# A gated-delta and mLSTM layer: branch a's gates projected beside branch b's, k's squares on ScalarE, two heads' w and state products in two banks

## The chip, the cores and the metric

One core of a Trainium2 chip runs the whole program. The metric is the device time of one execution in microseconds, the median of several executions. A profiled execution also leaves a trace; its span runs from the first to the last instruction.

## The reference

Two blocks follow each other on 256 tokens of width 1024. The first (two layers of token mixers and experts) is not touched. The second has two layers; in each, every product with a weight is over 1024 inputs:

```python
proj = x @ w_in      # q,k,v,o of branch a (mLSTM, 4 heads); q,k,v,z of branch b (gated delta, 8 heads); gate_a, gate_b
ha = headnorm(mlstm(qa, ka, va)) * sigmoid(oa)
q, k, v = silu(causal_conv(qkv_b))              # branch b; q, k then scaled by rsqrt(sum of squares + 1e-6)
# chunks of 64 tokens, per head: u, w from a triangular solve, then for each of 4 chunks
v_new = u - w @ S;  o = qe @ S + attn @ v_new;  S = S * g_end + kd.T @ v_new
hb = headnorm(o) * silu(zb)
y = sigmoid(gate_a) * (ha @ w_branch_a) + sigmoid(gate_b) * (hb @ w_branch_b)
x = layernorm(ALPHA * x + y @ w_out);  x = layernorm(ALPHA * x + ffn(x))
```

## The kernel before

Everything is in float32. A product with a weight matrix is made in `gemm_t` of three single-pass matmuls (lines L85 to L87): the weight tile `w` is split into a high and a low part `whl` (ScalarE copies the high part, L62, VectorE subtracts, L64), the activations are kept as such a pair (`xh`, `xl`). One call handles 256 output columns with 48 matmuls of 256 columns into one PSUM tile `acc`, and then an evacuation. Below, "projection matmul" is any of these. All other products (those in `gdn` and `mlstm`) are plain float32 matmuls, which the trace shows as two instructions each, transposes as one.

Branch b works on two heads at a time: a head pair `hp` holds its heads in the two halves of the 128 partitions (`halves`). `gdn_proj` projects q, k, v of a pair, applies the convolution, and GpSimd squares q and k (L1236, tiles `cva`). `gdn` then sums the squares over the 128 channels with matmuls against ones (`pss`, L1261), takes the reciprocal root, transposes k and v (`pk`, `pv`), scales k into `kt`, transposes it back (`pkT`), solves the triangular system in six levels (`pi`), makes u (`pu`) and w (`pw`, L1364), and walks the four chunks: `pO[:, 1]` is w times S (L1376), `vn` the new values (L1378), `pO[:, 0]` the output (L1380, L1393), `pS` the state product of each head (L1387), then VectorE updates S (L1389, L1391) and ScalarE takes the output and its squares out of PSUM (L1396, L1397). After the chunks comes the norm (L1406) and a transpose `pot` (L1409). PSUM tiles of a pair rotate through two banks (tag `ma` or `mb` by the parity of the pair).

`branches` makes the four gates of branch b (columns `GB`), the four products of hb with `w_branch_b`, and then by turns a gate of branch a (columns `GA`, into a tile `ta`) and a product of ha. The order of the steps is the string `ORDER2` (P and M: projections and core of branch a; G, Z and R: projections, gate and core of branch b; R0 to R3 twice, once a layer). That is the order of writing; a scheduler with its own timing then puts the instructions of each engine into their final order, and takes one that stands later when an earlier one has no free buffer or no data. Each engine executes its own list in that order.

Of the kernel before, what the change touches and what calls it, by code (L numbers as in the profile page):

```python
# [7 lines left out]
FT = mybir.dt.float32  # L8
FR = mybir.dt.float32r
I32 = mybir.dt.int32  # L10
AF = mybir.ActivationFunctionType
OP = mybir.AluOpType
# [31 lines left out]
def wload(E, parts, kn):  # L44

    nc = E.nc
    cols = sum(p.shape[1] for p in parts)
    w = E.wp.tile([128, kn, cols], FT, name="w", tag="w")
    o = 0
    for p in parts:  # L50
        n = p.shape[1]
        nc.sync.dma_start(w[:, :, o:o + n], p.rearrange("(k p) n -> p k n", p=128))
        o += n
    return w
# [18 lines left out]
def gemm_t(E, parts, xh, xl, evac, pool=None, tag="acc"):  # L73


    nc = E.nc
    j = 0
    for p in parts:
        for c in range(0, p.shape[1], 256):
            w = wload(E, [p[:, c:c + 256]], KC)  # L80
            ps = (pool or E.acc).tile([128, 2, 256], FT, name="acc", tag=tag)
            for b in range(2):
                h, lo = split(E, w[:, :, b * 128:(b + 1) * 128], [128, KC, 128])
                for k in range(KC):
                    nc.tensor.matmul(ps[:, b], h[:, k], xh[:, k], start=(k == 0), stop=False)  # L85
                    nc.tensor.matmul(ps[:, b], h[:, k], xl[:, k], start=False, stop=False)  # L86
                    nc.tensor.matmul(ps[:, b], lo[:, k], xh[:, k], start=False, stop=(k == KC - 1))  # L87
            evac(j, ps)
            j += 1
# [974 lines left out]
QA, KA, VA, OA, QB, KB, VB, ZB, GA, GB = 0, 512, 1024, 2048, 3080, 4104, 5128, 6152, 7192, 8216  # L1064
# [130 lines left out]
class G2:  # L1195
# [27 lines left out]
    def gdn_proj(self, hp):  # L1223
        E, nc, T, cw = self.E, self.E.nc, self.E.t2, self.cw
        z = Env()
        z.KQ = T.tile([128, 2, 4, 2, 64], FT, name="KQ")
        z.kr = T.tile([128, 4, 2, 64], FT, name="kr", bufs=1)
        z.vr = T.tile([128, 4, 2, 64], FT, name="vr", bufs=1)
        z.sq = []

        def ev(j, ps):
            dst = z.KQ[:, 1] if j == 0 else z.kr
            a = conv_piece(E, cw, j * 8 + 2 * hp, ps, dst)
            d2 = dst.rearrange("p c h t -> p (c h t)")
            z.sq.append(a.rearrange("p a b -> p (a b)"))
            nc.gpsimd.tensor_mul(z.sq[j], d2, d2)  # L1236
        gemm_t(E, [self.cols(QB + 256 * hp), self.cols(KB + 256 * hp)], self.xh, self.xl, ev)
        gemm_t(E, [self.cols(VB + 256 * hp)], self.xh, self.xl, lambda j, ps: conv_piece(E, cw, 16 + 2 * hp, ps, z.vr))
        return z
# [10 lines left out]
    def gdn(self, hp, z):  # L1250
        E, nc, m, C, T = self.E, self.E.nc, self.E.m, self.E.c2, self.E.t2
        gd, R, KQ = self.R["gd"], self.R, z.KQ
        p_ = "ab"[hp % 2]
        mt = "m" + p_
        halves = [slice(0, 64), slice(64, 128)]


        pss = m.tile([128, 2, 4], FT, name="pss", tag=mt)
        for j in range(2):
            for c in range(4):  # L1260
                nc.tensor.matmul(pss[:, j, c:c + 1], z.sq[j][:, c * 128:c * 128 + 128], C.ones[:, 0:1], start=True, stop=True)  # L1261
        nn = E.sm.tile([128, 8], FT, name="nn", tag="nn" + p_)
        nc.vector.tensor_scalar(nn, pss.rearrange("p a b -> p (a b)"), 1e-6, None, op0=OP.add)
        rr = E.sm.tile([128, 8], FT, name="rr", tag="rr" + p_)
        rsqrt(E, rr, nn, (128, 8), p_)
        qsc = E.sm.tile([128, 4], FT, name="qsc", tag="qsc" + p_)
# [1 line left out]
        rk = rr[:, 4:8]  # L1268


        pk = m.tile([128, 4, 128], FT, name="pk", tag=mt)
        pv = m.tile([128, 4, 128], FT, name="pv", tag=mt)
        for c in range(4):
            nc.tensor.transpose(pk[:, c], z.kr[:, c], C.id)
        for c in range(4):
            nc.tensor.transpose(pv[:, c], z.vr[:, c], C.id)
        kt = T.tile([128, 4, 128], FT, name="kt", bufs=1)
        nc.vector.tensor_mul(kt, pk, bc(rk, 128))
        vb = T.tile([128, 4, 128], FT, name="vb")
        nc.vector.tensor_mul(vb, pv, bc(gd[:, 1, hp], 128))  # L1280
# [2 lines left out]
        kd = T.tile([128, 4, 128], FT, name="kd")  # L1283
# [15 lines left out]
        ge = E.sm.tile([128, 2, 4], FT, name="ge", tag="ge" + p_)  # L1299
# [57 lines left out]
        u = vb  # L1357
        nc.scalar.activation(u, pu, AF.Copy)
        wT = kb.rearrange("p c (a b) -> p (c a) b", b=64).rearrange("p (h c) t -> p h c t", h=2)
        pws = []  # L1360
        for hpar, s in enumerate(halves):
            pw = m.tile([128, 4, 64], FT, name="pw", tag=mt)
            for c in range(4):
                nc.tensor.matmul(pw[:, c], kb[s, c], XY[s, 1, c], start=True, stop=True)  # L1364
            pws.append(pw)
        for hpar in range(2):
            nc.scalar.activation(wT[:, hpar], pws[hpar], AF.Copy)

# [1 line left out]
        ss = E.sm.tile([128, 4], FT, name="ss", tag="ss" + p_)  # L1370
        S = None
        for c in range(4):
            po = m.tile([128, 2, 128], FT, name="pO", tag=mt)
            if c:
                for hpar, s in enumerate(halves):
                    nc.tensor.matmul(po[s, 1], wT[:, hpar, c], S[:, hpar], start=True, stop=True, skip_group_check=True)  # L1376
                vn = T.tile([128, 128], FT, name="vn", tag="vn" + p_, bufs=1)
                nc.vector.tensor_sub(vn, u[:, c], po[:, 1])  # L1378
                for hpar, s in enumerate(halves):
                    nc.tensor.matmul(po[s, 0], qe[:, c, hpar], S[:, hpar], start=True, stop=False, skip_group_check=True)  # L1380
            else:
                vn = u[:, 0]
            if c < 3:
                Sn = T.tile([128, 2, 128], FT, name="S", tag="S" + p_, bufs=2)
                for hpar, s in enumerate(halves):
                    pS = m.tile([128, 128], FT, name="pS", tag=mt)
                    nc.tensor.matmul(pS, kd[s, c], vn[s], start=True, stop=True)  # L1387
                    if c:
                        nc.vector.scalar_tensor_tensor(Sn[:, hpar], S[:, hpar], ge[:, hpar, c:c + 1], pS, op0=OP.mult, op1=OP.add)  # L1389
                    else:  # L1390
                        nc.vector.tensor_copy(Sn[:, hpar], pS)  # L1391
            for s in halves:
                nc.tensor.matmul(po[s, 0], at[s, c], vn[s], start=(c == 0), stop=True, skip_group_check=True)  # L1393
            if c < 3:
                S = Sn
            nc.scalar.activation(u[:, c], po[:, 0], AF.Copy)  # L1396
            nc.scalar.activation(self.junk[:, 0:128], po[:, 0], AF.Square, accum_out=ss[:, c:c + 1])  # L1397


        nc.vector.tensor_mul(ss, ss, qsc)  # L1400
# [124 lines left out]
    def branches(self):  # L1525

        E, nc, T = self.E, self.E.nc, self.E.t2
        l = self.l
        self.yh = E.st.tile([128, 8, 256], FR, name="yh", tag="st")
        self.yl = E.st.tile([128, 8, 256], FR, name="yl", tag="st")  # L1530
        yb = []

        def gate(c0, p, t):
            gemm_t(E, [self.cols(c0 + 256 * p)], self.xh, self.xl,
                   lambda j, ps: nc.scalar.activation(t, ps, AF.Tanh, scale=0.5))

        def product(p):
            t = yb[p]
            gemm_t(E, [E.i["w_branch_b_2"][l, :, 256 * p:256 * p + 256]], self.hbh, self.hbl,
                   lambda j, ps: nc.vector.scalar_tensor_tensor(t, t, 1.0, ps, op0=OP.add, op1=OP.mult))  # L1540
        for p in range(4):
            t = E.rows.tile([128, 2, 256], FT, name="yb", tag="yg", bufs=3) if p < 3 else T.tile([128, 2, 256], FT, name="yb", tag="vb")
            yb.append(t)
            gate(GB, p, t)
        for p in range(4):
            product(p)
        for p in range(4):
            f = slice(2 * p, 2 * p + 2)
            t = T.tile([128, 2, 256], FT, name="ta", tag="gs")
            gemm_t(E, [self.cols(GA + 256 * p)], self.xh, self.xl,  # L1550
                   lambda j, ps: nc.scalar.activation(t, ps, AF.Tanh, scale=0.5))

            def ev(j, ps):
                y = T.tile([128, 2, 256], FT, name="cva")
                nc.vector.scalar_tensor_tensor(y, t, 1.0, ps, op0=OP.add, op1=OP.mult)
                nc.vector.tensor_add(y, y, yb[p])
                nc.scalar.activation(self.yh[:, f], y, AF.Copy, scale=0.5)
                nc.vector.scalar_tensor_tensor(self.yl[:, f], y, 0.5, self.yh[:, f], op0=OP.mult, op1=OP.subtract)
            gemm_t(E, [E.i["w_branch_a_2"][l, :, 256 * p:256 * p + 256]], self.hah, self.hal, ev)
# [310 lines left out]
```

## Time and profile before

| | |
|---|---|
| median of 3 executions | 2811.3 us (2809.31 to 2815.72) |
| profiled execution | 2815.0 us, span 2813.3 us |
| TensorE (PE) busy in the span | 2524.8 us, 90% |
| VectorE (DVE), ScalarE (ACT), GpSimd (POOL) busy | 1350.2, 821.7 and 239.6 us |
| mean granted clock of TensorE | 0.958 |

The share of busy time is a mean over both blocks. The second block starts at about 1520 us; its two layers are the stretches to read. PE's weight loads have a row of their own (PEld) and overlap the matmuls. A granted clock of 1.00 is 2.4 GHz, 0.50 is 1.2 GHz.

### The profile page before, as it was taken

What the parts mean: (1) busy time and instruction counts of PE and PEld (TensorE: products, weight loads), DVE (VectorE), ACT (ScalarE), POOL (GpSimd) and SP (SyncE); (2) the same over time, 40 slices, a digit from 0 to 9 for tenths busy, and PEclk for the clock granted to TensorE, in tenths of its full rate; (3) what the DMA queues carried; (4) which work ended last, traced back from release to release, by engine and by line L of the source; (5) the groups of instructions that cost most, each with busy time, mean ns of one, the idle gap of its engine ahead of it and who ended that gap; (6) DMA issues with size and microseconds to landing.
All of it is one profiled execution on the core that took longest, in us unless ns stands there. A gap on an engine that the chain in (4) does not pass through costs nothing.

```text
span 2813.3 us, 42526 instructions
## 1 busy us (share of the span) xinstructions
PE 2524.8 (90%) x17783; PEld 1736.5 (62%) x17783; DVE 1350.2 (48%) x2673; ACT 821.7 (29%) x1343; POOL 239.6 (9%) x309
## 2 busy tenths in 40 slices
PE   6999989988889998666667999999999999999998
PEld 4776733322227662111114988888997898879996
DVE  4446533232236562001103767456655677455765
ACT  2334310000014440000002434334444443334442
POOL 1000010000000001000000122000201031100200
PEclk8999999999999999998899998999999998999999
DMA  7534469999995468999997421335654431235553
GB/s 294 180 120 148 165 265 421 421 421 421 421 384 197 168 250 370 421 421 421 421 421 280 152 92 53 113 111 177 209 181 139 150 121 46 94 102 198 178 193 120
DMA packets 237460, 665.61 MB, mean 237 GB/s; under 512 B 11572, under 2 KB 165860, under 8 KB 182356
## 3 DMA queue, kind: packets, MB, share of 16 engines
q1 hardware_dynamic: 235428, 657.81, 61.4%
q0 software_dynamic: 1696, 4.59, 0.5%
q8 instruction: 140, 2.29, 0.3%
q10 hardware_dynamic: 144, 0.49, 0.1%
q14 instruction: 52, 0.43, 0.0%
HBM read 661.78 MB, written 1.05 MB: 236 GB/s over the span
## 4 chain that ended last, share of the span: by engine, by line
PE 60%; DMA 24%; issue 9%; DVE 4%; POOL 2%; ACT 1%; SPq 0%; DVEq 0%; ACTq 0%; POOLq 0%
DMA w<-in_exp_w_up 9%; DMA w<-in_exp_w_down 8%; PE acc L85 6%; PE acc L87 6%; PE acc L86 6%; DMA w<-in_exp_w_gate 6%; PE pj L317 3%; PE pj L319 3%; PE pj L318 3%; PE pgate L883 3%; PE pd L883 3%; PE pup L883 2%; PE pada L183 2%; PE psc L436 1%; PE psc L452 1%
## 5 line engine op out<-in xcount | busy, mean ns | idle before, releaser
L64 DVE TENSOR_TENSOR whl<-w,whl 128x1024 fp32r<-128x1024 f32 x376 | 469.0, 1251 | 297.6 <-ACT whl L62 296.7
L62 ACT ACTIVATE whl<-w 128x1024 fp32r<-128x1024 f32 x376 | 396.1, 1058 | 483.5 <-PE acc L87 245.0
L85 PE MATMUL acc<-xh,whl 128*128 128x256 f32 x1664 | 474.4, 285 | 0.8 <-DVE xh L1648 0.5
L86 PE MATMUL acc<-xl,whl 128*128 128x256 f32 x1664 | 471.1, 283 | 0.0
L87 PE MATMUL acc<-xh,whl 128*128 128x256 f32 x1664 | 470.5, 283 | 0.2
L85 PEld LDWEIGHTS acc<-xh,whl 128*128 128x128 f32 x1664 | 315.1, 189 | 10.4 <-issue 6.3
L86 PEld LDWEIGHTS acc<-xl,whl 128*128 128x128 f32 x1664 | 315.2, 189 | 5.0 <-issue 3.9
L87 PEld LDWEIGHTS acc<-xh,whl 128*128 128x128 f32 x1664 | 314.8, 189 | 5.3 <-issue 3.3
L883 PE MATMUL pup<-w,xg 128*64 128x512 f32 (+1 forms) x1024 | 223.6, 665 | 68.6 <-DMA w<-in_exp_w_up 68.6
L883 PE MATMUL pd<-w,ehT 128*64 128x512 f32 (+1 forms) x1024 | 208.3, 639 | 58.1 <-DMA w<-in_exp_w_down 41.0
L883 PE MATMUL pgate<-w,xg 128*64 128x512 f32 (+1 forms) x1016 | 215.2, 635 | 47.3 <-DMA w<-in_exp_w_gate 38.7
L883 PEld LDWEIGHTS pup<-w,xg 128*64 128x64 f32 (+1 forms) x1024 | 52.0, 129 | 231.1 <-DMA w<-in_exp_w_up 151.4
L883 PEld LDWEIGHTS pd<-w,ehT 128*64 128x64 f32 (+1 forms) x1024 | 52.4, 127 | 188.8 <-DMA w<-in_exp_w_down 85.7
L883 PEld LDWEIGHTS pgate<-w,xg 128*64 128x64 f32 (+1 forms) x1016 | 50.9, 126 | 176.7 <-DMA w<-in_exp_w_gate 84.0
L317 PE MATMUL pj<-whl,hT 128*128 128x256 f32 x496 | 144.5, 292 | 5.9 <-ACT hT L301 5.8
L319 PE MATMUL pj<-whl,hT 128*128 128x256 f32 x496 | 143.1, 289 | 1.1 <-DVE hT L302 1.1
L318 PE MATMUL pj<-whl,hT 128*128 128x256 f32 x496 | 143.0, 289 | 0.0
L914 DVE TENSOR_TENSOR od<-pd,g 128x512 f32<-128x512 f32 x24 | 16.6, 691 | 237.7 <-PE pd L883 237.7
L902 DVE SCALAR_TENSOR_TENSOR et<-et,pup 128x512 f32<-128x512 f32 x24 | 16.5, 686 | 227.7 <-PE pup L883 227.5
L317 PEld LDWEIGHTS pj<-whl,hT 128*128 128x128 f32 x496 | 94.4, 190 | 23.7 <-issue 10.0
L318 PEld LDWEIGHTS pj<-whl,hT 128*128 128x128 f32 x496 | 94.5, 191 | 11.6 <-issue 5.9
L319 PEld LDWEIGHTS pj<-whl,hT 128*128 128x128 f32 x496 | 94.2, 190 | 9.5 <-issue 6.5
(610 smaller groups left out, 4148.3 us busy)
## 6 DMA issues: line engine op xcount, KB each, us to landing
w<-in_exp_w_down SPq DMA_DIRECT2D x128, 1024.0 KB, 19.8
w<-in_exp_w_up SPq DMA_DIRECT2D x127, 1024.0 KB, 19.8
w<-in_exp_w_gate SPq DMA_DIRECT2D x125, 1024.0 KB, 19.8
w<-in_w_in SPq DMA_DIRECT2D x82, 1024.0 KB, 5.0
w<-in_ada_w SPq DMA_DIRECT2D x48, 1024.0 KB, 6.5
w<-in_w_ffn_up SPq DMA_DIRECT2D x44, 1024.0 KB, 5.1
w<-in_w_ffn_down SPq DMA_DIRECT2D x22, 1024.0 KB, 4.9
w<-in_w_out SPq DMA_DIRECT2D x16, 1024.0 KB, 6.2
```

Source lines behind the costliest of these rows:

```text
L62: nc.scalar.activation(h, w, AF.Copy)
L64: (engine or nc.vector).tensor_sub(lo, w, h)
L85: nc.tensor.matmul(ps[:, b], h[:, k], xh[:, k], start=(k == 0), stop=False)
L86: nc.tensor.matmul(ps[:, b], h[:, k], xl[:, k], start=False, stop=False)
L87: nc.tensor.matmul(ps[:, b], lo[:, k], xh[:, k], start=False, stop=(k == KC - 1))
L183: nc.tensor.matmul(self.ps[32 * j:32 * j + 32], self.st[:, k], ws[j], start=(k == 0), stop=(k == KC - 1), skip_group_check=True)
L317: nc.tensor.matmul(ps, xh, wh, start=start, stop=False, skip_group_check=bool(ks))
L318: nc.tensor.matmul(ps, xh, wl, start=False, stop=False, skip_group_check=bool(ks))
L319: nc.tensor.matmul(ps, xl, wh, start=False, stop=stop, skip_group_check=bool(ks))
L436: self.E.nc.tensor.matmul(o, wT[:, 128 * c:128 * c + 128], v[:, t0 + c, 64 * h:64 * h + 64], start=(c == 0), stop=(c == n // 128 - 1))
L452: nc.tensor.matmul(ps[:, :n], self.cqT[r, h // 2, 128 * t:128 * t + 128], self.ckT[r, h // 2, k0:k0 + n], start=True, stop=True)
L883: m = nc.tensor.matmul(ps[64 * h + mw * i:64 * h + mw * i + mw], lhs(kk, i, e), ws[i][k][:, 512 * h:512 * h + 512], start=(kk == 0), stop= ...
```

## The change

GpSimd squares q alone. k is transposed first, into `pk`; ScalarE squares `pk` chunk by chunk and sums along the free axis into `nn` (the squares themselves go to `kt`, which is overwritten later). The matmuls against ones are left for q. The loop of the w products runs over chunks outside and heads inside. The state product of the first head of a pair goes to a third part of `pO`, that of the second to `pS`, and both are issued ahead of the two updates of S. The squares of the output are read from `u` in SBUF. In `branches`, all four gates of branch a come after those of branch b and ahead of the products, into the places of `kr`, `vr`, `cvt` and `kt`.

```diff
@@ gdn_proj
-            z.sq.append(a.rearrange("p a b -> p (a b)"))
-            nc.gpsimd.tensor_mul(z.sq[j], d2, d2)
+            if j == 0:
+                z.sq = a.rearrange("p a b -> p (a b)")
+                nc.gpsimd.tensor_mul(z.sq, d2, d2)
@@ gdn
-        pss = m.tile([128, 2, 4], FT, name="pss", tag=mt)
-        for j in range(2):
-            for c in range(4):
-                nc.tensor.matmul(pss[:, j, c:c + 1], z.sq[j][:, c * 128:c * 128 + 128], C.ones[:, 0:1], start=True, stop=True)
+        pk = m.tile([128, 4, 128], FT, name="pk", tag=mt)
+        for c in range(4):
+            nc.tensor.transpose(pk[:, c], z.kr[:, c], C.id)
+        pss = m.tile([128, 4], FT, name="pss", tag=mt)
+        for c in range(4):
+            nc.tensor.matmul(pss[:, c:c + 1], z.sq[:, c * 128:c * 128 + 128], C.ones[:, 0:1], start=True, stop=True)
...
+        kt = T.tile([128, 4, 128], FT, name="kt", bufs=1)
+        for c in range(4):
+            nc.scalar.activation(kt[:, c], pk[:, c], AF.Square, accum_out=nn[:, 4 + c:5 + c])
+        nc.vector.tensor_copy(nn[:, 0:4], pss)
+        nc.vector.tensor_scalar(nn, nn, 1e-6, None, op0=OP.add)
...
-        for hpar, s in enumerate(halves):
-            pw = m.tile([128, 4, 64], FT, name="pw", tag=mt)
-            for c in range(4):
+        pws = [m.tile([128, 4, 64], FT, name="pw", tag=mt) for _ in halves]
+        for c in range(4):
+            for pw, s in zip(pws, halves):
                 nc.tensor.matmul(pw[:, c], kb[s, c], XY[s, 1, c], start=True, stop=True)
...
-            po = m.tile([128, 2, 128], FT, name="pO", tag=mt)
+            po = m.tile([128, 3, 128], FT, name="pO", tag=mt)
...
-                for hpar, s in enumerate(halves):
-                    pS = m.tile([128, 128], FT, name="pS", tag=mt)
-                    nc.tensor.matmul(pS, kd[s, c], vn[s], start=True, stop=True)
+                pS = [po[:, 2], m.tile([128, 128], FT, name="pS", tag=mt)]
+                for hpar, (p, s) in enumerate(zip(pS, halves)):
+
+                    nc.tensor.matmul(p, kd[s, c], vn[s], start=(hpar == 1 or c == 0), stop=True, skip_group_check=True)
+                for hpar, p in enumerate(pS):
...
-            nc.scalar.activation(self.junk[:, 0:128], po[:, 0], AF.Square, accum_out=ss[:, c:c + 1])
+            nc.scalar.activation(self.junk[:, 0:128], u[:, c], AF.Square, accum_out=ss[:, c:c + 1])
@@ branches
+        ta = []
+        for p, tag in enumerate(("kr", "vr", "cvt", "kt")):
+            ta.append(T.tile([128, 2, 256], FT, name="ta", tag=tag, bufs=1))
+            gate(GA, p, ta[p])
         for p in range(4):
             product(p)
         for p in range(4):
             f = slice(2 * p, 2 * p + 2)
-            t = T.tile([128, 2, 256], FT, name="ta", tag="gs")
-            gemm_t(E, [self.cols(GA + 256 * p)], self.xh, self.xl,
-                   lambda j, ps: nc.scalar.activation(t, ps, AF.Tanh, scale=0.5))
+            t = ta[p]
```

What the scheduler makes of it shows in the lists of TensorE. In these rows a float32 matmul counts once, `pi` is the triangular solve, L85 to L87 are projection matmuls; the changed kernel's line numbers are up to four higher. First, layer 0, the end of the last pair's chunks (R3), before:

```order
L1380 MATMUL pO<-S,qe 64x128 x2
L1393 MATMUL pO<-vn,at__12322 64x128 x2
L1409 MATMUL pot<-cst_98,vb 128x128 x4
L1517 MATMUL pha<-cst_98,nm 128x128
L1457 MATMUL pb<-row_MS,cst_98 128x512
```

and in the changed kernel, where "..." stands for further projection matmuls:

```order
L1380 MATMUL pO<-S,qe 64x128 x2
L1395 MATMUL pO<-vn,at__12313 64x128 x2
L85 MATMUL acc<-xh,whl 128x256
L86 MATMUL acc<-xl,whl 128x256
L87 MATMUL acc<-xh,whl 128x256
...
L1411 MATMUL pot<-cst_98,vb 128x128 x4
```

Between the last output product and `pot` there was nothing and there are now 72 projection matmuls of branch a's gates; in layer 1 there were 18, and there are 72.

Second, layer 0, the chunks of the second pair (R1) and the start of the next pair, before:

```order
L1380 MATMUL pO<-S,qe 64x128 x2
L1393 MATMUL pO<-vn,at__10527 64x128 x2
L1387 MATMUL pS<-vb,kd 128x128 x2
L1393 MATMUL pO<-vb,at__10932 64x128 x2
L1376 MATMUL pO<-S,kb 64x128 x2
L1380 MATMUL pO<-S,qe 64x128 x2
L1387 MATMUL pS<-vn,kd 128x128
L1393 MATMUL pO<-vn,at__10932 64x128 x2
L1387 MATMUL pS<-vn,kd 128x128
L1376 MATMUL pO<-S,kb 64x128
L1409 MATMUL pot<-cst_98,vb 128x128 x4
L1261 MATMUL pss<-cst_98,cva 128x1 x8
```

and in the changed kernel, where "..." stands for projection matmuls:

```order
L1376 MATMUL pO<-S,kb 64x128 x2
...
L1380 MATMUL pO<-S,qe 64x128 x2
L1388 MATMUL pO<-vn,kd 128x128
L1388 MATMUL pS<-vn,kd 128x128
L1411 MATMUL pot<-cst_98,vb 128x128 x4
L1260 MATMUL pk<-cst_98,kr 128x128 x4
L1395 MATMUL pO<-vn,at__10929 64x128 x2
L1376 MATMUL pO<-S,kb 64x128 x2
L1263 MATMUL pss<-cst_98,cva 128x1 x4
```

The two state products of a chunk now stand next to each other, the first in `pO`; `pss` has half its matmuls; and the "..." is 15 projection matmuls where the product with w was followed by its consumer at once.

Third, layer 0, u and w of the first pair (R0), in the changed kernel:

```order
L1358 MATMUL pu<-vb,XY 64x128 x8
L1365 MATMUL pw<-XY,kb 128x64 x4
L1346 MATMUL pi<-T_11016,XY 64x64 x3
L1350 MATMUL pi<-XY,T_11016 64x64 x8
L87 MATMUL acc<-xh,whl 128x256
L1365 MATMUL pw<-XY,kb 128x64 x4
```

The four products of one head still stand together, other work comes between, and the other head's four follow, as before: `pu` and the two `pw` rotate through two banks.

## Rows read from the trace of the kernel before

**Rows 1.** Windows: busy us of each engine, granted clock (PEclk), DMA share, GB/s.
```profile
core 0: us, PE busy (x) PEld busy (x) DVE busy (x) ACT busy (x) POOL busy (x), PEclk, DMA share, GB/s
...
1520.00:2813.00 1293.00, 1250.96 (x10461) 1112.72 (x10460) 811.28 (x1459) 534.16 (x810) 179.13 (x184) 0.97 0.41 136
```

**Rows 2.** PE's waits from 1520 us on: total us, times, longest.
```profile
PE pot L1409 <- DVE vb L1406: 7.7, 4, 4.5
...
PE pO L1380 <- DVE vn L1378: 1.7, 4, 0.5
```

**Rows 3.** PE timeline, last state chains: start us, us, engine, line, tiles [idle before].
```profile
1856.66 0.43 PE L1393 MATMUL pO<-vn,at__12322 64*64 64x128 f32 x4
1861.58 1.11 PE L1409 MATMUL pot<-cst,vb 128*128 128x128 f32 x4 [4.49 <-DVE vb L1406]
...
2509.14 0.91 PE L1409 MATMUL pot<-cst,vb 128*128 128x128 f32 x4 [2.19 <-DVE vb L1406]
```

**Rows 4.** Windows cut where the granted clock changes (columns as in rows 1).
```profile
1860.90:1871.10 10.20, 9.08 (x33) 6.96 (x34) 6.07 (x14) 2.72 (x4) 1.82 (x2) 0.50 0.00 0
2509.40:2516.20 6.80, 6.16 (x21) 4.03 (x20) 3.52 (x9) 2.04 (x4) 1.82 (x2) 0.50 0.00 0
1686.80:1700.50 13.70, 12.97 (x61) 10.46 (x62) 10.04 (x41) 3.96 (x11) 0.00 (x0) 0.50 0.00 0
2338.70:2348.90 10.20, 10.17 (x47) 8.79 (x46) 7.54 (x26) 3.31 (x8) 0.00 (x0) 0.50 0.00 1
1734.60:1741.40 6.80, 6.42 (x73) 5.47 (x70) 6.54 (x17) 2.67 (x6) 1.02 (x2) 0.50 0.01 4
2383.10:2389.90 6.80, 6.46 (x74) 5.52 (x71) 6.54 (x18) 2.66 (x6) 1.12 (x2) 0.50 0.01 2
```

**Rows 5.** PE timeline: last projection matmuls before a stretch without them, first one after.
```profile
1676.93 0.28 PE L86 MATMUL acc<-xl,whl 128*128 128x256 f32 x1
1677.05 0.28 PE L87 MATMUL acc<-xh,whl 128*128 128x256 f32 x1
...
1697.78 0.56 PE L85 MATMUL acc<-xh,whl 128*128 128x256 f32 x1
```

**Rows 6.** PE timeline, norm products and what follows, at full and at half clock.
```profile
1585.46 0.95 PE L1261 MATMUL pss<-cst,cva 128*128 128x1 f32 x8
1586.34 0.71 PE L1482 MATMUL pd<-vm,kw 64*128 64x258 f32 x4
...
1693.05 3.41 PE L1261 MATMUL pss<-cst,cva 128*128 128x1 f32 x16
1696.39 0.69 PE L1376 MATMUL pO<-S,kb 128*64 128x128 f32 x2
```

**Rows 7.** PE timeline, a state product alone, then two heads' one after the other.
```profile
1666.99 0.49 PE L1387 MATMUL pS<-vb,kd 64*128 64x128 f32 x2
1667.41 0.38 PE L85 MATMUL acc<-xh,whl 128*128 128x256 f32 x1
1667.63 0.28 PE L86 MATMUL acc<-xl,whl 128*128 128x256 f32 x1
...
1789.08 0.49 PE L1387 MATMUL pS<-vb,kd 64*128 64x128 f32 x4
1789.50 0.68 PE L1339 MATMUL pi<-XY,Am 64*64 64x64 f32 x16
```

**Rows 8.** PE timeline, one head's w products and what follows.
```profile
1661.56 1.10 PE L1364 MATMUL pw<-XY,kb 64*128 64x64 f32 x8
1662.59 0.39 PE L85 MATMUL acc<-xh,whl 128*128 128x256 f32 x1
```

**Rows 9.** Lines L1397 and L1236: duration ns min/median/max, first and last start.
```profile
L1397 ACT ACTIVATE junk<-pO x32: 267/272/278, 1670.7 to 2504.9; 128x128 f32<-128x128 f32 x32
L1397 ACT ACTIVATION_READ_ACCUMULATOR junk<-pO x32: 202/204/213, 1670.8 to 2505.0; 128x1 f32 x32
...
L1236 POOL TENSOR_TENSOR cva<-kr x8: 1040/1040/1041, 1589.3 to 2374.6; 128x512 f32<-128x512 f32 x8
```

More of the change, by code (lines that the diff above doesn't have):

```diff
@@ L1228, in gdn_proj @@
         z.vr = T.tile([128, 4, 2, 64], FT, name="vr", bufs=1)
-        z.sq = []
         def ev(j, ps):
@@ L1255, in gdn @@
         halves = [slice(0, 64), slice(64, 128)]
-        pss = m.tile([128, 2, 4], FT, name="pss", tag=mt)
-        for j in range(2):
-            for c in range(4):
-                nc.tensor.matmul(pss[:, j, c:c + 1], z.sq[j][:, c * 128:c * 128 + 128], C.ones[:, 0:1], start=True, stop=True)
-        nn = E.sm.tile([128, 8], FT, name="nn", tag="nn" + p_)
-        nc.vector.tensor_scalar(nn, pss.rearrange("p a b -> p (a b)"), 1e-6, None, op0=OP.add)
+        pk = m.tile([128, 4, 128], FT, name="pk", tag=mt)
[4 more added lines that the diff above has]
+            nc.tensor.matmul(pss[:, c:c + 1], z.sq[:, c * 128:c * 128 + 128], C.ones[:, 0:1], start=True, stop=True)
+        nn = E.sm.tile([128, 8], FT, name="nn", tag="nn" + p_)
+        kt = T.tile([128, 4, 128], FT, name="kt", bufs=1)
[3 more added lines that the diff above has]
+        nc.vector.tensor_scalar(nn, nn, 1e-6, None, op0=OP.add)
         rr = E.sm.tile([128, 8], FT, name="rr", tag="rr" + p_)
@@ L1268, in gdn @@
         rk = rr[:, 4:8]
-        pk = m.tile([128, 4, 128], FT, name="pk", tag=mt)
         pv = m.tile([128, 4, 128], FT, name="pv", tag=mt)
         for c in range(4):
-            nc.tensor.transpose(pk[:, c], z.kr[:, c], C.id)
-        for c in range(4):
             nc.tensor.transpose(pv[:, c], z.vr[:, c], C.id)
-        kt = T.tile([128, 4, 128], FT, name="kt", bufs=1)
         nc.vector.tensor_mul(kt, pk, bc(rk, 128))
@@ L1359, in gdn @@
         wT = kb.rearrange("p c (a b) -> p (c a) b", b=64).rearrange("p (h c) t -> p h c t", h=2)
-        pws = []
-        for hpar, s in enumerate(halves):
-            pw = m.tile([128, 4, 64], FT, name="pw", tag=mt)
-            for c in range(4):
+        pws = [m.tile([128, 4, 64], FT, name="pw", tag=mt) for _ in halves]
+        for c in range(4):
+            for pw, s in zip(pws, halves):
                 nc.tensor.matmul(pw[:, c], kb[s, c], XY[s, 1, c], start=True, stop=True)
-            pws.append(pw)
         for hpar in range(2):
@@ L1384, in gdn @@
                 Sn = T.tile([128, 2, 128], FT, name="S", tag="S" + p_, bufs=2)
-                for hpar, s in enumerate(halves):
-                    pS = m.tile([128, 128], FT, name="pS", tag=mt)
-                    nc.tensor.matmul(pS, kd[s, c], vn[s], start=True, stop=True)
+                pS = [po[:, 2], m.tile([128, 128], FT, name="pS", tag=mt)]
+                for hpar, (p, s) in enumerate(zip(pS, halves)):
+                    nc.tensor.matmul(p, kd[s, c], vn[s], start=(hpar == 1 or c == 0), stop=True, skip_group_check=True)
+                for hpar, p in enumerate(pS):
                     if c:
-                        nc.vector.scalar_tensor_tensor(Sn[:, hpar], S[:, hpar], ge[:, hpar, c:c + 1], pS, op0=OP.mult, op1=OP.add)
+                        nc.vector.scalar_tensor_tensor(Sn[:, hpar], S[:, hpar], ge[:, hpar, c:c + 1], p, op0=OP.mult, op1=OP.add)
                     else:
-                        nc.vector.tensor_copy(Sn[:, hpar], pS)
+                        nc.vector.tensor_copy(Sn[:, hpar], p)
             for s in halves:
```

## The prediction

> **What bounds the kernel now.** I first read the page's slices and then cut the span into windows. The second block, from 1520 us on, is where all edits lie. In it PE is busy 1251.0 of 1293 us, DVE 811, ACT 534, POOL 179, and the DMA engines 0.41 of the time [rows 1]. So PE bounds this block: a matmul that goes away shortens it by its own length, while work on the other engines costs only where PE waits for it. There are three things to look for, then: what PE executes, where it waits, and at which clock it runs.
>
> The waits of PE name few places [rows 2]. The largest is `pot`, the transpose at the end of a head pair: 7.7 us in four waits. Two of these stand at the ends of the layers' last chunks, 4.49 and 2.19 us [rows 3]. In layer 0 the last product ends at 1857.1 and `pot` starts at 1861.6: ScalarE's squares, the root and the scaling of the norm pass while PE has nothing else, because the products with `w_branch_b` need this very head pair.
>
> The clock hangs on the same places. Six windows in the two layers' head-pair phases ran at half clock, 1.2 GHz, with PE busy almost throughout [rows 4]. The reader is to see what stands ahead of them: one follows each of the two long waits, the other four fall in stretches in which small products stand alone. The longest such stretch in layer 0 holds no projection matmul from 1677.05 to 1697.78 [rows 5], and its clock fell at 1686.8. What half clock costs shows in one kind of instruction: eight `pss` instructions take 0.88 us (1585.46 to 1586.34), sixteen take 3.34 us at half clock (1693.05 to 1696.39), so 1.67 for eight [rows 6]. Of busy time at half clock, 1 - 0.88/1.67 = 0.47 is lost.
>
> **The change part by part.** The sum is made against the profiled execution, 2815.0 us (span 2813.3), which is 3.7 above the median of 2811.3.
>
> *Squares of k.* Each of the 8 head pairs loses 4 matmuls, eight instructions, 0.88 us of PE [rows 6]: 8 x 0.88 = **-7.0 us**. Added are 32 squares on ACT, priced by the nearest row, the squares of the output: 0.272 for the square and 0.204 for reading the sum, 15.2 us in all [rows 9], on an engine that is busy 41% of the block. POOL loses 8 x 1.04 us. The latency grows: four squares, 1.9 us, and a DVE copy, where one POOL instruction of 1.04 us and a product stood. What waits behind it is `kt`, and behind that `pkT`. In the order of the changed kernel at least 50 projection matmuls stand between `pk` and `pkT` of every pair; at 0.12 us each [rows 5] that is 6 us of cover. I cost it at nothing; were the cover gone, it would be up to 8 x 1.9 = 15 us.
>
> *State products.* A product alone holds PE for 0.42 us (1666.99 to 1667.41); two heads' products one behind the other also hold it for 0.42 (1789.08 to 1789.50) [rows 7]. The second is free. The Trainium skill, TensorEngine Tiling (Array Packing), "Restrictions and Gotchas", has the rule for it: different row tiles write to different PSUM banks and can't access one bank at a time; the pair here is in two banks and overlaps, so the trace agrees. By counting the order, the 48 products before were 7 pairs and 34 alone, 41 slots; now they are 17 pairs and 14 alone, 31 slots, for the pairs of chunks 1 and 2 all stand together and those of chunk 0 mostly no longer do. 10 x 0.42 = **-4.2 us** (up to -6 where a slot alone also makes the next projection matmul start late, 0.22 instead of 0.12 after the one before it [rows 5, 7]).
>
> *w products.* One head's four take 1.03 us [rows 8]. Alternating between the heads could halve that, 8 x 1.03 = -8.2 us. But the order of the changed kernel still has all four of one head, then other work, then the four of the other: `pu` and two `pw` share two banks, so the second `pw` waits until ScalarE has emptied `pu`. I take **0**.
>
> *Squares of the output from SBUF.* They free the PSUM tile one square, 0.27 us, earlier [rows 9]. It is no work of PE: 0.
>
> *Gates of branch a ahead of the products.* The work is the same, 48 matmuls a gate, and the weights come in the same sizes at 0.41 of the DMA engines' time [rows 1]. What moves is cover. Between the last output product and `pot` there are now 72 projection matmuls in both layers, 8.6 us at 0.12 each, against waits of 4.49 and 2.19: these 6.7 us go. So do the half-clock windows behind them, 9.08 + 6.16 = 15.2 us busy [rows 4], worth 0.47 x 15.2 = 7.2. Together **-13.9 us**. The ha chain of the last mLSTM head, which had gates to hide behind, now has 31 projection matmuls, 3.7 us, ahead of its first reader; the three steps between, on DVE, ACT and DVE, each take a 128x512 tile, for which the slowest engine needs 1.04 us [rows 9], so at most 3.1, and nothing is late there.
>
> The same gates let projections move up into the earlier phases. The start of the third pair and the first mLSTM core (windows at 1734.6 and 2383.1, busy 6.42 + 6.46) had no projection matmul and now have runs of 29, 9 and 18 in layer 0, similar ones in layer 1: 0.47 x 12.9 = 6.1, and the two shorter waits of `pot`, 7.7 - 6.7 = 1.0, make **-7.1 us**. The chunks of the second pair (windows at 1686.8 and 2338.7, busy 12.97 + 10.17) are interleaved with projections too, but in each layer a dense stretch of about 6 us of small products remains (an estimate: the order's rows by their times in the trace). The bounds are 0 and 0.47 x 23.1 + 1.7 (the waits of `pO` for `vn` [rows 2]) = -12.6. As 6 us is nearer to the 6.8 us of the window at 1734.6 [rows 4] than to none, I take a third, **-4.2 us**.
>
> *What is new.* Projections cut into more slices: by count, projections are entered after a matmul of another tile shape 149 times, before 133. The skill's page on tiling ("Tiling Modes") says that a change of tiling mode drains TensorE, which speaks against this change; rows 7 show the late start after such a change. By rows 5 and 7, 16 x 0.10 = 1.6 us; bounds 0 and 16 x 0.42 = 6.7. I take **+2 us**.
>
> Sum: -7.0 - 4.2 + 0 - 13.9 - 7.1 - 4.2 + 2 = -34.4. That is 2780.6 against 2815.0, and 2776.9 against the median.
>
> **The rivals.** *The clock does not come back:* only work and the long waits go, -7.0 - 4.2 - 6.7 + 2 = -15.9, 2795. For it: small products remain dense around R1 and around the mLSTM core. Against: the windows behind the long waits have a cause that goes. *All of it comes back:* the chunks of the second pair run at full clock too, -34.4 - 8.4 = -42.8, and the cut slices cost nothing, -44.8: 2766 to 2768. For it: no stretch without projections is left that is half as long as the 20.7 us of rows 5. *Two banks for w:* if the two heads' products did overlap, -8.2 more, 2769 alone; the order contradicts it. *ScalarE's squares hold the pairs up:* +15 on the forecast, 2792; against it stand the 50 matmuls. *Slower:* the cut slices keep the clock down. If projections in runs of ten to twenty between small products no longer lift it, half clock spreads over the phases of the pairs, some 640 us in both layers. To end 5.6 us above the median it must lose 34.4 + 5.6 = 40 us, 40/0.47 = 85 us of busy time at half clock beyond the 15 that the forecast leaves, where all six windows had 51.3. Against it: before, every return to projections ended a half-clock window within about 3 us (1697.78 to 1700.5 [rows 4, 5]).
>
> **How the numbers follow.** Forecast 0.54; all comes back 0.17; clock does not come back 0.13; squares hold up 0.06; w overlaps 0.02; a mixture of losses that cancels the gain 0.04; slower 0.04. About 0.2%, 5.6 us, is what a measurement of this kernel can tell from no change. The predicted time is 2777. The range of 8 in 10 is 2763 to 2796: the lower end is all comes back with a little of the state products' upper bound, the upper end is the rival without the clock. Faster by over 0.2%: 0.92, within 0.2%: 0.04, slower: 0.04.
>
> **What the profile would show.** Right: `pss` with 64 instructions fewer; no wait of `pot` over 1 us; no half-clock window at the ends of the last chunks and around the first mLSTM core; state products of chunks 1 and 2 as rows of four instructions of 0.49 us; `pw` still in eights of 1.1 us. Wrong: PE waiting at `pkT` or in `acc` for ScalarE's split behind a square; half-clock windows of more than 25 us in all in the pairs' phases; a new wait ahead of the first product of ha.

## The result and the profile after

The changed kernel takes 2775.5 us (median of 4 runs, 2771.2 to 2778.5) against 2813.5 for the kernel before (median of 4, 2809.3 to 2820.0). The ratio is 0.9856, with an interval of 0.9841 to 0.987. The forecast was 2777.

First the windows of the changed kernel, for comparison with [rows 1] and [rows 4] (same columns): the whole second block, then the windows of the pairs' phases in which the granted clock was 1.2 GHz.

```profile
1520.00:2771.80 1251.80, 1216.57 (x10387) 1088.11 (x10386) 809.31 (x1463) 543.79 (x872) 171.33 (x176) 0.98 0.42 139
1553.80:1557.20 3.40, 3.40 (x16) 3.40 (x17) 0.30 (x2) 0.00 (x0) 0.00 (x0) 0.50 0.00 0
1704.00:1710.80 6.80, 6.80 (x36) 5.76 (x34) 6.63 (x26) 2.38 (x6) 0.00 (x0) 0.50 0.00 0
...
2222.80:2229.60 6.80, 6.01 (x28) 6.04 (x29) 6.34 (x23) 2.14 (x4) 1.73 (x2) 0.50 0.00 0
2349.10:2352.50 3.40, 3.40 (x21) 3.01 (x16) 2.88 (x11) 1.24 (x3) 2.78 (x4) 0.50 0.10 39
```

PE is busy 34.4 us less than in [rows 1], and the half-clock windows of these phases shrink from 54.5 us [rows 4] to 20.4. The waits of PE, against [rows 2]:

```profile
PE pln L1646 <- ACT x L1639: 7.4, 3, 2.5
PE va L93 <- ACT qT L1427: 4.0, 1, 4.0
PE acc L85 <- DVE dn L1506: 2.5, 1, 2.5
```

`pot` is gone from the list, and a wait of 2.5 us for `dn` is new. PE's timeline at the end of the last chunks of layer 0, where [rows 3] had 4.49 us of waiting:

```profile
1840.73 0.44 PE L1395 MATMUL pO<-vn,at__12313 64*64 64x128 f32 x4
1841.10 0.39 PE L87 MATMUL acc<-xh,whl 128*128 128x256 f32 x1
...
1849.57 0.28 PE L86 MATMUL acc<-xl,whl 128*128 128x256 f32 x1
1849.69 0.60 PE L1411 MATMUL pot<-cst,vb 128*128 128x128 f32 x4
```

Projection matmuls fill the 8.6 us from 1841.1 to `pot`. The next lines are two heads' state products in two banks, and then one head's w products (PE timeline again):

```profile
1703.62 0.37 PE L1388 MATMUL pO<-vn,kd 64*128 64x128 f32 x1
1703.63 0.37 PE L1388 MATMUL pS<-vn,kd 64*128 64x128 f32 x1
1703.84 0.27 PE L1388 MATMUL pO<-vn,kd 64*128 64x128 f32 x1
1703.84 0.27 PE L1388 MATMUL pS<-vn,kd 64*128 64x128 f32 x1
1704.05 1.12 PE L1279 MATMUL pv<-cst,vr 128*128 128x128 f32 x4
```

```profile
1687.46 1.10 PE L1365 MATMUL pw<-XY,kb 64*128 64x64 f32 x8
1688.50 0.44 PE L1395 MATMUL pO<-vn,at__10526 64*64 64x128 f32 x4
```

The instructions of the two heads start within 0.01 us of each other, and the next product starts 0.43 after the first: two products in the 0.42 that one alone takes [rows 7]. One head's w still takes 1.04 [rows 8].

The prediction doesn't count another product of the chunks that changes with them, w times S in `pO[:, 1]`. First one head's in the kernel before, then both heads' in the changed kernel, each with what follows it:

```profile
1677.67 0.43 PE L1376 MATMUL pO<-S,kb 128*64 128x128 f32 x2
1678.04 0.68 PE L1339 MATMUL pi<-XY,Am 64*64 64x64 f32 x16
...
1837.20 0.44 PE L1376 MATMUL pO<-S,kb 128*64 128x128 f32 x4
1837.57 0.39 PE L86 MATMUL acc<-xl,whl 128*128 128x256 f32 x1
```

One head alone holds PE for 0.37 us, and so do two together. Counted in the traces, 8 of the 24 pairs stood together before and the other 32 products alone, 40 slots; now all 24 stand together. That is 16 slots, 16 x 0.37 = 5.9 us.

The squares of k on ACT (durations in ns, as in [rows 9]) cost what the squares of the output cost:

```profile
L1267 ACT ACTIVATE kt<-pk x32: 259/277/298, 1593.9 to 2359.4; 128x128 f32<-128x128 f32 x32
L1267 ACT ACTIVATION_READ_ACCUMULATOR kt<-pk x32: 193/206/230, 1594.0 to 2359.6; 128x1 f32 x32
```

### The profile page after: what moved, and what is told of

Read it like the earlier page. It is cut to its first block, busy times and chain, and to the rows that moved or that the text cites. A ratio compares the mean times of both kernels' runs of the same rounds, so it can differ in the third digit from the quotient of the medians.

```text
span 2771.8 us, 42425 instructions
## 1 busy us (share of the span) xinstructions
PE 2489.7 (90%) x17719; PEld 1711.0 (62%) x17719; DVE 1350.3 (49%) x2681; ACT 832.8 (30%) x1407; POOL 231.2 (8%) x301
## 4 chain that ended last, share of the span: by engine, by line
PE 60%; DMA 25%; issue 8%; DVE 3%; POOL 2%; ACT 1%; SPq 1%; DVEq 0%; ACTq 0%; POOLq 0%
DMA w<-in_exp_w_down 10%; DMA w<-in_exp_w_up 8%; PE acc L85 7%; PE acc L86 7%; PE acc L87 7%; DMA w<-in_exp_w_gate 6%; PE pj L317 3%; PE pj L319 3%; PE pj L318 3%; PE pgate L883 3%; PE pd L883 2%; PE pup L883 2%; PE pada L183 2%; PE psc L436 1%; PE psc L452 1%
## 5 line engine op out<-in xcount | busy, mean ns | idle before, releaser
L85 PE MATMUL acc<-xh,whl 128*128 128x256 f32 x1664 | 475.9, 286 | 4.0 <-DVE dn L1506 2.5
L87 PE MATMUL acc<-xh,whl 128*128 128x256 f32 x1664 | 473.8, 285 | 0.0
L85 PEld LDWEIGHTS acc<-xh,whl 128*128 128x128 f32 x1664 | 317.8, 191 | 15.1 <-issue 8.6
L87 PEld LDWEIGHTS acc<-xh,whl 128*128 128x128 f32 x1664 | 317.5, 191 | 6.6 <-issue 4.7
```

## The experiments

Two theories stand against each other. **By edit:** each edit earns its own term, as the prediction booked them (gates about -23 with the new slices, squares -7, state products -4). **By cover:** there is one stock of projection matmuls that the scheduler lays between small products; an edit that moves or shortens a chain of small products decides where this stock is left over, so that the value of an edit depends on the others.

For each run the windows of the second block, from its first matmul (`pln`) to PE's last, give PE's busy time. The column "rest" is the length less that; it is mostly waiting. "Half clock" is the sum of the windows at 1.2 GHz in the pairs' phases, as in [rows 4]; "at half clock" is PE's busy time in all windows at 1.2 GHz of the whole block. "Ahead of `pot`" counts the projection matmuls between the last output product of a layer's last pair and `pot`, in layers 0 and 1. "Pairs" counts, of 24, the state products that stand as two heads together, or where one follows the other at once, and "w S" does the same for w times S. One profile stands behind each row, and the ratios come from the timed runs.

| kernel | ratio to before | block, us | PE busy | rest | half clock | at half clock | ahead of `pot` | pairs | w S |
|---|---|---|---|---|---|---|---|---|---|
| before | | 1282.3 | 1252.5 | 29.8 | 54.5 | 64.4 | 0, 18 | 7 | 8 |
| gates_only | 0.9942 | 1266.1 | 1242.9 | 23.3 | 30.7 | 50.8 | 80, 70 | 7 | 8 |
| squares_only | 1.0007 | 1280.8 | 1241.5 | 39.3 | 37.4 | 51.8 | 0, 0 | 2 | 11 |
| state_only | 0.9899 | 1261.1 | 1238.5 | 22.6 | 30.6 | 55.3 | 41, 41 | 19 | 24 |
| no_gates | 0.9887 | 1252.7 | 1221.7 | 31.0 | 17.0 | 38.4 | 19, 41 | 17 | 24 |
| no_squares | 0.9891 | 1254.8 | 1233.8 | 21.0 | 37.5 | 51.6 | 81, 81 | 19 | 24 |
| no_state | 0.9932 | 1269.7 | 1240.3 | 29.4 | 23.8 | 47.0 | 80, 70 | 1 | 9 |
| after | 0.9856 | 1244.1 | 1219.7 | 24.4 | 20.4 | 37.5 | 72, 72 | 17 | 24 |

### Each part alone

*Gates alone.*

```diff
+        ta = []
+        for p, tag in enumerate(("kr", "vr", "cvt", "kt")):
+            ta.append(T.tile([128, 2, 256], FT, name="ta", tag=tag, bufs=1))
+            gate(GA, p, ta[p])
         for p in range(4):
             product(p)
```

> The kernel before with branch a's gates moved ahead of the products, nothing else. The prediction's booking (the gates cover the ends of the last chunks and also let projections into the second pair's chunks and the first mLSTM core): 13.9 + 7.1 + 4.2 = 25 us faster than before. The rival (the gates cover only the ends of the last chunks; the order of this kernel still has the second pair's chunks and the mLSTM core without projections): 14 us faster, with the half-clock windows around 1687, 1735, 2339 and 2383 us still there.

Measured: 2799.9 us, ratio 0.9942 (0.9927 to 0.9957), about -16. The ends of the last chunks are covered: of the 7.7 us of waits at `pot` [rows 2] 1.2 are left. The dense stretch of the second pair is not (windows, layers 0 and 1, against the third and fourth of [rows 4]):

```profile
1691.90:1705.60 13.70, 13.09 (x61) 10.58 (x62) 10.05 (x40) 3.96 (x11) 0.00 (x0) 0.50 0.00 0
2333.60:2343.80 10.20, 10.12 (x46) 8.82 (x47) 7.50 (x25) 3.43 (x8) 0.00 (x0) 0.50 0.00 1
```

So the gates take the waits and the clock behind them, but they put no projections into the second pair. The windows at 1735 and 2383, which the rival kept, are gone, although the order there is that of before (see the last section), and two new ones of 3.4 us stand at 1558.8 and 2255.1: part of the 16 us is clock that this order doesn't explain. The -4.2 that the prediction booked there under the gates isn't theirs.

*Squares of k alone.*

```diff
-        for j in range(2):
-            for c in range(4):
-                nc.tensor.matmul(pss[:, j, c:c + 1], z.sq[j][:, c * 128:c * 128 + 128], C.ones[:, 0:1], start=True, stop=True)
+        for c in range(4):
+            nc.tensor.transpose(pk[:, c], z.kr[:, c], C.id)
...
+            nc.scalar.activation(kt[:, c], pk[:, c], AF.Square, accum_out=nn[:, 4 + c:5 + c])
```

> The kernel before with the squares of k on ScalarE alone. The prediction's booking: 7 us faster, the removed products alone. The rival (the new place of k's transposes and squares makes the scheduler put projections between the small products of the second pair and of the mLSTM core): 15 to 20 us faster, with the half-clock windows there gone or shorter, and the waits at the ends of the last chunks as before.

Measured: 2817.8 us, ratio 1.0007 (0.9996 to 1.0017). PE loses 11.0 us of busy time, and the rest grows by 9.4. Where the rest grew shows in its waits, and in PE's timeline at the end of both layers:

```profile
PE pot L1411 <- DVE vb L1408: 10.0, 3, 4.5
...
PE pha L1519 <- POOL nm L1515: 3.9, 6, 1.3
PE acc L85 <- DVE dn L1506: 2.5, 1, 2.5
```

```profile
1861.72 0.44 PE L1395 MATMUL pO<-vn,at__12322 64*64 64x128 f32 x4
1866.65 1.12 PE L1411 MATMUL pot<-cst,vb 128*128 128x128 f32 x4 [4.50 <-DVE vb L1408]
...
2504.34 0.44 PE L1395 MATMUL pO<-vn,at__18873 64*64 64x128 f32 x4
2509.26 1.12 PE L1411 MATMUL pot<-cst,vb 128*128 128x128 f32 x4 [4.49 <-DVE vb L1408]
```

The last pair's chunks of layer 0 hold 105 projection matmuls where they held 157, and layer 1 has none of its 18 left at the end, which waits 4.49 instead of 2.19. They stand earlier, and the half-clock windows of the second pair's chunks are gone. Gain and loss come from the same projections in another place, which speaks for the cover.

*State products with the squares of the output.*

```diff
-            po = m.tile([128, 2, 128], FT, name="pO", tag=mt)
+            po = m.tile([128, 3, 128], FT, name="pO", tag=mt)
...
+                pS = [po[:, 2], m.tile([128, 128], FT, name="pS", tag=mt)]
...
-            nc.scalar.activation(self.junk[:, 0:128], po[:, 0], AF.Square, accum_out=ss[:, c:c + 1])
+            nc.scalar.activation(self.junk[:, 0:128], u[:, c], AF.Square, accum_out=ss[:, c:c + 1])
```

> The kernel before with the state products in two banks and the output's squares read from SBUF alone. The prediction's booking: 4 us faster (up to 6). The rival (the shorter chain of the chunks also shortens the dense stretches and their half-clock windows): 9 us faster or more. If two heads' products do not overlap: no change.

Measured: 2789.3 us, ratio 0.9899 (0.9881 to 0.9917), about -28, where the booking had -4.2. The timeline of the end of layer 0 shows where it comes from:

```profile
1842.92 0.44 PE L1395 MATMUL pO<-vn,at__12313 64*64 64x128 f32 x4
1843.29 0.38 PE L86 MATMUL acc<-xl,whl 128*128 128x256 f32 x1
...
1849.30 0.28 PE L87 MATMUL acc<-hbh,whl 128*128 128x256 f32 x1
1849.42 0.60 PE L1411 MATMUL pot<-cst,vb 128*128 128x128 f32 x4
```

From the first to the last output product of this pair's four chunks it is 25.9 us with 157 projection matmuls in before, and 19.2 us with 118 here. The other 41 are left for the end, where `pot` waited 4.49 [rows 3] and now doesn't wait. Nearly the same stock is laid elsewhere. At 0.12 us each, the 39 projections that are gone from the chunks are 4.7 of these 6.7 us; the chain's own part is about 2. That the scheduler moves them because the chain is shorter is the likely reason; no run shows it.

The sum over the whole block: 12 more pairs of state products at 0.42 make 5.0, the 16 slots of w times S 5.9, the rest falls by 7.2, and 9.1 us less of busy time at half clock make 0.47 x 9.1 = 4.3. Together 22.4, and the block is 21.2 shorter. So half of the 21.2 are slots of PE, of which the prediction counted the smaller part, and the other half are waits and clock.

### Each part taken out

The same hunks as above, taken out of the changed kernel one at a time. For the gates:

```diff
-        ta = []
-        for p, tag in enumerate(("kr", "vr", "cvt", "kt")):
-            ta.append(T.tile([128, 2, 256], FT, name="ta", tag=tag, bufs=1))
-            gate(GA, p, ta[p])
...
-            t = ta[p]
+            t = T.tile([128, 2, 256], FT, name="ta", tag="gs")
```

> The changed kernel with the gates of branch a by turns with its products, as before. The prediction's booking: 25 us of the gain go with the gates, so 13 us faster than before. The rival (the gates cover the ends of the last chunks alone): 14 us go, so 24 faster than before, with the waits of the transpose at the ends of the last chunks back.

For the squares of k:

```diff
-        for c in range(4):
-            nc.scalar.activation(kt[:, c], pk[:, c], AF.Square, accum_out=nn[:, 4 + c:5 + c])
-        nc.vector.tensor_copy(nn[:, 0:4], pss)
```

> The changed kernel with the squares of k on GpSimd and the products against ones, as before. The prediction's booking: 7 us of the gain go, so 31 us faster than before. The rival (the place of k's transposes and squares lets the projections in): 18 us go, so 20 faster than before, with half-clock windows in the second pair's chunks.

For the state products and the squares of the output:

```diff
-            po = m.tile([128, 3, 128], FT, name="pO", tag=mt)
+            po = m.tile([128, 2, 128], FT, name="pO", tag=mt)
```

> The changed kernel with the state products in one bank after the other and the output's squares read from PSUM, as before. The prediction's booking: 4 us of the gain go (up to 6), so 32 to 34 us faster than before. The rival (a shorter chain of the chunks): 9 us or more go, so under 29.

Measured: 2785.1 (ratio 0.9887, 0.9866 to 0.9907), 2786.7 (0.9891, 0.9871 to 0.991) and 2798.8 (0.9932, 0.991 to 0.9953). Against the changed kernel's 0.9856 the gates are worth 0.31% in company, the squares 0.35% and the state products 0.76%, or 9, 10 and 21 us; each of these differences is uncertain by some 0.25%. Alone they were worth 16, 0 and 28. For the squares the difference between alone and in company is beyond the intervals. For the other two it has the sign that a shared stock asks for, but it is within what the runs can tell. Both ways the three add up to the whole (1.52% and 1.42%, against 1.44%). Against what was expected: without the gates it is still 32 us faster than before, more than the booking (13) and its rival (24) had; without the squares it is 31, as booked; without the state products it is 19, as their rival had it (under 29).

### The state products and the squares of the output apart

```diff
+                pS = [po[:, 2], m.tile([128, 128], FT, name="pS", tag=mt)]
```

> The kernel before with the state products in two banks alone; the output's squares are read from PSUM as before. In its order 17 of 24 state products stand in pairs (7 before), projections are entered from another tile shape 127 times (133 before), and 20 projection matmuls stand ahead of the transpose at the end of the last chunks (0 and 18 before). If the two banks are the cause of the state edit's 28 us: 20 us faster than before or more. If reading the squares from SBUF, which frees the PSUM tile of a chunk earlier, is the larger part: under 10 us.

```diff
-            nc.scalar.activation(self.junk[:, 0:128], po[:, 0], AF.Square, accum_out=ss[:, c:c + 1])
+            nc.scalar.activation(self.junk[:, 0:128], u[:, c], AF.Square, accum_out=ss[:, c:c + 1])
```

> The kernel before with the output's squares read from SBUF alone. If the two banks are the cause of the state edit's gain: no change within 3 us. If the earlier release of the PSUM tile is: 10 us faster or more.

Two banks alone: 2794.6 us, ratio 0.9933 (0.9908 to 0.9957), -19. Squares from SBUF alone: 2818.1, ratio 1.0012 (0.9998 to 1.0025), no gain. The last four chunks of layer 0 take 21.0 us with 133 projection matmuls with two banks alone, and 26.1 with 156 with the squares alone. So it is the two banks that change the order, and w times S stands in 24 pairs with them and in 8 without. The 19 us are just short of the 20 that the expectation asked for, and the interval (12 to 26) holds both. The waits at the end of layer 0, first with two banks alone, then with the squares alone:

```profile
1855.03 0.44 PE L1411 MATMUL pot<-cst,vb 128*128 128x128 f32 x2 [1.97 <-DVE vb L1408]
```

```profile
1866.53 1.12 PE L1409 MATMUL pot<-cst,vb 128*128 128x128 f32 x4 [4.67 <-DVE vb L1406]
```

Together the two edits give -28 and no wait there. That is more than their sum, but the intervals of 0.9899 and 0.9933 overlap, and the profiled blocks of the two kernels are equally long (1261.1 and 1260.8 us): whether the squares help once the two banks are there stays open.

### The w products really in two banks

With the w edit alone the order of every engine is that of before, row by row, and without it that of the changed kernel. So the edit as it stands changes nothing; no run was made of it alone. Here the second head's tile comes from the tag of the projections:

```diff
-        pws = [m.tile([128, 4, 64], FT, name="pw", tag=mt) for _ in halves]
+        pws = [m.tile([128, 4, 64], FT, name="pw", tag=t) for t in (mt, "mm")]
```

> The changed kernel with the second head's w products in a bank of the tag mm, so that both heads' products can start together; the order has 54 places where the heads alternate, the changed kernel none. If two heads' w products overlap as the state products do: 8 us faster than the changed kernel, 46 faster than before, and a head pair's sixteen w instructions in about 1.1 us. If they do not overlap, their weight loads being as wide as in one head's run: as the changed kernel, 38 faster than before. If the bank is missed by the mLSTM core: slower than the changed kernel.

It was run twice, the second time beside the changed kernel itself:

> The changed kernel with the second head's w products in a bank of the tag mm, once more, in more rounds. By the count of its instructions, 7 us of TensorE's time fewer than the changed kernel. If that arrives: 45 us faster than before and 7 faster than the changed kernel beside it. If new waits take it back, as the first comparison leaves open: 0 to 3 faster than the changed kernel.

> The changed kernel itself, beside the next one on one chip: 38 us faster than before.

Measured: 2772.3 us, ratio 0.9844 (0.983 to 0.9859); then 2771.5, ratio 0.985 (0.9827 to 0.9873), beside 2774.1, ratio 0.9865 (0.9842 to 0.9888). It is the fastest of all that ran, by 2.6 us beside the changed kernel on one chip, but the intervals overlap. PE's timeline of one pair, in the second of these runs, and its new waits:

```profile
1660.90 1.11 PE L1365 MATMUL pw<-XY,kb 64*128 64x64 f32 x16
1661.94 0.56 PE L1346 MATMUL pi<-T,XY 64*64 64x64 f32 x12
```

```profile
PE acc L85 <- DVE rst_a L39: 3.4, 2, 1.7
PE acc L85 <- ACT whl L62: 3.1, 2, 1.6
PE pe L1300 <- DVE H L1306: 1.7, 1, 1.7
PE pot L1411 <- DVE vb L1408: 1.6, 2, 1.3
```

Both heads' products take 1.04 us, where one head's took 1.03 [rows 8]: over the eight pairs PE's time for `pw` falls by 8.0 us, as the prediction's rival had it. Beside the changed kernel's profile of the same chip, PE's busy time falls by 8.8 (1219.0 to 1210.2) and the rest grows by 3.2 (26.7 to 30.0); the waits above are new or longer, and the one for `dn` is not there. These two executions are 5.3 us apart, the medians 2.6. So the products overlap, part of the gain goes into new waits, and how much of it is left is within what the runs can tell.

## Why the prediction was right, and where it was not

**The sum.** It had -34.4 against the profiled execution, with -9.2 in matmuls (-7.0 - 4.2 + 2) and -25.2 in waits and clock (13.9 + 7.1 + 4.2). The block became 38.2 shorter, PE's busy time fell by 32.8 and the rest by 5.4. The half-clock windows of the pairs' phases hold 19.6 us of busy time where they held 51.3, which by the prediction's 0.47 is 14.9, against 16.9 forecast (7.2 + 6.1 + 3.6). Over the whole block it is 37.5 where it was 64.4, worth 12.6, since other windows grew. Of the 32.8 that leaves 20.2 for matmuls at full clock, 11.0 more than forecast. Counting finds 17.1: 64 `pss` (7.0), ten state slots (4.2), and the 16 slots of w times S (5.9), which the prediction left out. The last 3.1 are not attributed, and the rest fell by 5.4 where 8.3 were forecast (6.7 + 1.0 + 0.6). So 5.9 us that were overlooked stand against waits and clock that gave some 7 us less: that the median came out within 2 us of the forecast is in part luck.

**The booking was wrong.** The step that failed is "10 x 0.42 = -4.2 us" for the state products. It counted the slots of the state products alone. It left out that w times S of the two heads comes together with them (5.9 us), and that the chunks then hold fewer projections, which are left for the end, where they remove the same waits that the prediction gave to the gates. Measured it is 28 us alone and 21 in company. The gates, booked at -25.2 less the new slices' 2, are worth 16 alone and 9 in company. The squares, booked at -7.0, are worth nothing alone and 10 in company. The waits at the ends of the last chunks go with the gates, and without them also with the state products (0.3 us is left at `pot` in state_only); the prediction counted them once, under the gates, which is right for the sum and not for the parts. That a shared stock makes the whole difference between alone and in company is not shown: beyond the intervals it stands for the squares only.

**Squares "at nothing".** The matmuls went as forecast (64 instructions). The new order was not free. The four kernels of the table with this edit have the wait of PE for `dn` in layer 1, 2.5 us, and the four without it don't; in the changed kernel a half-clock window of 6.8 us begins in it. The timelines of PE, ACT and DVE in the changed kernel, in that order, show the queue:

```profile
2220.46 0.66 PE L1499 MATMUL pn<-Cn,qs 128*64 128x258 f32 x4
2223.59 0.55 PE L85 MATMUL acc<-xh,whl 128*128 128x256 f32 x1 [2.48 <-DVE dn L1506]
```

```profile
2220.12 0.27 ACT L1267 ACTIVATE kt<-pk 128x128 f32<-128x128 f32 x1
...
2221.03 0.23 ACT L1267 ACTIVATION_READ_ACCUMULATOR kt<-pk 128x1 f32 x1
2221.12 0.50 ACT L1182 ACTIVATE cva<-acc,cw 128x256 f32<-128x256 f32 x1
2221.47 0.42 ACT L1501 ACTIVATE nm<-pn 128x258 f32<-128x258 f32 x1
```

```profile
2222.51 0.15 DVE L1505 SCALAR_TENSOR_TENSOR dn<-nm 128x2 f32<-128x2 f32 x1
2222.58 0.86 DVE L1185 SCALAR_TENSOR_TENSOR cva<-acc,cw,cva 128x254 f32<-128x254 f32 x2
...
2223.44 0.15 DVE L1506 TENSOR_TENSOR dn<-dn,col 128x2 f32<-128x2 f32 x1
```

`nm` stands behind the four squares and a piece of the convolution on ACT, but its input `pn` is done on PE only at 2221.12, so they hold it back by 0.35 us at most. The larger part is on DVE: `nm` is done at 2221.89, the first step of `dn` starts at 2222.51, and the convolution stands between it and the second, which ends at 2223.59. So the price is that of an order in which the pair's work and the mLSTM core meet; the two runs with the w products really in two banks have the squares on ScalarE too, but not this wait. With 0.47 of the window's 6.01 us busy time it is about 5.3 us. The prediction looked for the squares' price at `pkT`, and for ScalarE's split; it appears at the mLSTM core that now stands behind `pk`. Its bound of 15 us held. The squares' own time was priced too high: squares and readings overlap, the four take 1.14 us (2220.12 to 2221.26) where the prediction had 1.9, and ACT's busy time in the block grows by 9.6 us instead of 15.2.

**The clock.** "No half-clock window at the ends of the last chunks" held in both layers, and at the two places that the prediction names with the first mLSTM core (1734.6 and 2383.1) none is left. New are the windows at 1553.8 and at 2222.8, the latter at the mLSTM head that comes first in layer 1. The forecast left about 15 us of busy time at half clock in the pairs' phases; 19.6 are left, in 17 to 20 us of windows over two profiles. The rival in which the clock does not come back is out, and so is the slower one. The price per window was too high in one place: from the second pair's last `pot` to the first projection behind it, the same 100 instructions in the same order took 10.41 us in before, with its window at half clock (1729.90 to 1740.31), and 8.91 in gates_only at full clock (1734.93 to 1743.84). These 1.5 us stand against the 2.5 that the prediction's price makes of the window's part in this stretch (0.47 x 5.33 busy): at full clock PE waits there 0.7 us more for DVE and ACT. One reading of the prediction does not hold: not every return to projections ended a half-clock window within about 3 us. In the window at 1860.9 [rows 4] the first projection came at 1865.54, and half clock lasted for another 5.6 us, until 1871.1.

**The w products** at 0 were right, for the reason given: the order keeps the heads apart. The new slices (+2) were not measured apart. Their price of 0.10 us a return is seen, but not as one of the tile shape: in before, at full clock, the second projection starts 0.20 us after the first when products of the full 128 rows and columns stood ahead (28 returns, median), 0.22 after other tile shapes (120 returns), and 0.12 within a run.

## What to carry to other kernels

A product that goes off a dependent chain can be worth more than its slot: count which other products then come together, ask what the scheduler will put where the chain was, and which wait further on that work will cover. Where several edits draw on one stock of filler work, forecast them together, with the stock counted once; the value of an edit measured alone can then differ from its value in company (here the squares of k, 0 and 10 us). An alternation in the code is only a wish while both tiles rotate through one pair of banks: read it off the order.

## What the runs showed of the hardware beyond this

**The clock does not follow from the order of PE alone.** The stretch behind `pot` of the second pair has the same matmuls in the same order in before and gates_only; before ran it at 1.2 GHz, in the windows at 1734.6 and 2383.1 [rows 4], gates_only at 2.4 (windows of the same place, layers 0 and 1):

```profile
1739.60:1746.40 6.80, 5.72 (x88) 4.65 (x83) 6.80 (x21) 2.72 (x7) 1.05 (x2) 1.00 0.01 4
2377.90:2384.70 6.80, 5.72 (x88) 4.66 (x86) 6.77 (x22) 2.64 (x7) 1.13 (x2) 1.00 0.01 2
```

Two executions of the changed kernel differ likewise: 1704.0 to 1710.8 at half clock in the first, at full clock in the second, which has its window at 1690.3 instead:

```profile
1690.30:1693.70 3.40, 3.40 (x20) 2.51 (x18) 0.00 (x0) 0.02 (x2) 0.29 (x1) 0.50 0.00 0
1704.00:1710.80 6.80, 6.03 (x54) 4.68 (x54) 6.31 (x24) 2.65 (x8) 0.00 (x0) 1.00 0.00 0
```

The Trainium skill, TensorE: Matmul & The Clock Gate, Part 1 ("What's actually happening"), says of a kernel's first matmuls that how many of them run slow varies from run to run; these rows show the like in mid-kernel. Which of the windows fall is left open here, and so is why those of gates_only did not.

**Two heads' products also overlap with 64 columns moving.** Sixteen instructions of `pw` in two banks take 1.04 us, as eight do in one. The Trainium skill, TensorEngine Tiling (Array Packing), "Restrictions and Gotchas", wants different row tiles in different banks; w and state products, at 64 and 128 moving columns, both agree with it. The two heads of w times S, which write the two partition halves of one tile `pO`, overlap as well: 0.37 us for both.
